# An encoder trunk on one core: the gated attention output turned by transposing DMAs instead of TensorE, and the joins of turned tiles queued behind weight casts

## The chip, the cores and the metric

The kernel runs on one core of one Trainium2 chip. The metric is the device time of one execution in microseconds. All times "at" some point are microseconds from the start of the profiled span. The engines are TensorE (PE, its weight loads PEld), VectorE (DVE), ScalarE (ACT), GpSimd (POOL) and SyncE (SP), which here only issues DMAs.

## The reference

256 tokens of width 1024 go through two layers. What matters here:

```python
u = rms_norm(h, g_mix_pre)
(gq, gk, gv, gg, ra_f, ra_b, aq, ak, av, gate_a, gate_b) = jnp.split(u @ w_in, offsets, axis=-1)
...
o_gla = rms_norm(o_f + o_b, g_gla_out).reshape(b, s, GLA_VAL).astype(h.dtype)
branch_a = (o_gla * jax.nn.silu(gg)) @ w_o_gla
...
branch_b = gqa_attention(q, k, v) @ w_o_attn
mixed = jax.nn.sigmoid(gate_a) * branch_a + jax.nn.sigmoid(gate_b) * branch_b
h = h + rms_norm(mixed @ w_out, g_mix_post)
```

Then follow a gated FFN of 2816 hidden units (`w_ffn_in`, silu, `w_ffn_out`), its norm and residual, and the layer's input embedding, `h += rms_norm(sigmoid(h @ w_ple_gate) * (p[i] @ w_ple_proj))`. Everything is 32-bit floating point.

## The kernel before, in words

**Tiles and precision.** The tokens are two halves (`hf` 0 and 1) of 128 partitions. A matmul takes its activations turned, 128 features on the partitions by the tokens, as the stationary operand; the weights stream as the moving operand, 512 columns at a time. To keep 32-bit accuracy each operand is split (`split`, L132 to 134) into a high part, a cast on ACT, and a low part, a subtraction on DVE; a product is three matmuls (high x high, high x low, low x high), so that one 512-column result of four 128-feature steps is a group of 12 matmuls. `Split` holds a turned activation: its high and low tiles, and `makers`, the tasks that still have to make parts of it.

**Weights.** `Stream` (L248 on) brings the weights in units of 1 MB: a DMA on SP's queue into `raw` (two buffers; some units of the gates and the FFN go into `lent` or `big` tiles), then two casts into `wh` on ACT and two subtractions into `wl` on DVE (`fill`, `made`, four buffers each). Gate B and pairs of FFN blocks are computed with seven products in place of eight (`seven`, L713; the sums of weights stand on L326 to L332).

**Order of the work.** The program is traced in one order, and a scheduler places each engine's instructions by it, by priorities (`tc.high_priority`) and by `tc.issue_after`, which puts an instruction behind a named one on the same engine. A `Task` (its code is a generator) is work for later: it yields a number of ticks, and a `tick` comes after every six matmuls or so of the main stream, 1.36 us. What it makes is demanded at the latest by `need`, where a matmul uses it.

**Turning by TensorE.** `transpose_in` (L445) turns 128 x 128 blocks by TensorE (L449) into a PSUM tile `aux`, and splits it from there (L134). The gated output of branch A is made in `out_gate` (L1451): `sg`, the sigmoid of `gg`, times `gg` and `on`, one 128 x 1024 tile for each half. `turn_in` (L557) makes a task that turns it after `W["g"]` = 6 ticks, into `gT`, which the first merge unit (`w_o_gla`) multiplies. Four tiles of four transposes per layer, `aux_0gg` and `aux_1gg`.

**Turning by DMA.** The FFN's hidden activations `hid` are turned by a DMA (`turned` L1573, `turn_out` L455, `take_in` L472), which handles only 16-bit elements: ACT copies a 32-bit tile into two planes of its upper and lower halves (L468), SP issues one `dma_start_transpose` (L469, 128 x 8 x 128 elements), and after `WAIT_TURNED` = 9 ticks ACT joins the turned planes into 32-bit values (L476), which are then split. Planes and turned planes lie in halves of a fresh `mid` tile. Block pairs make one such tile for each half (k = 4, 12, 16); the last pair (k = 16) is turned by TensorE. Single blocks (k = 0, 8, 10, 20) have both halves in one tile or, for the first, one tile for each half.

## Time and profile before

| | |
|---|---|
| median of three runs | 908.5 us (908.41 to 908.8) |
| the profiled execution's own time | 909.68 us |
| its span | 907.9 us |
| granted clock of TensorE | 0.999 |

The span is the stretch from the first to the last recorded instruction; the profiled execution took 1.8 us more than its span and 1.2 us more than the median. A row of the timeline gives the start, the time until the end of the last of its instructions, the engine, the line, the operation, the tiles (without their numbers) and the count; in square brackets stands how long the engine was idle before it, and what ended the wait. Matmuls overlap in the pipeline, so their cost is read from the distance of starts.

### The profile page before, as it was taken

Reading aid. Unit: us, or ns where it says so; the run is one execution under the profiler, and the core shown is the slowest. Engines: PE = TensorE matmul, PEld = TensorE weight load, DVE = VectorE, ACT = ScalarE, POOL = GpSimd, SP = SyncE. Lnnn points to the kernel's source line nnn. Section 1 sums busy time; section 2 is a strip of 40 time slices with the busy share of each in tenths; the row PEclk is TensorE's granted clock in tenths of the full one; section 3 lists DMA queues with packets and bytes.
Section 4 is the critical chain, followed back from the end, with each engine's and each line's share of the span. In section 5 each row is a group of like instructions: output and inputs, shape, how many; then the busy total and the mean of one; then the engine's idle time right before and its main releaser. Section 6 shows DMA issues by size and latency. Waiting matters only on the chain.

```text
span 907.9 us, 12157 instructions
## 1 busy us (share of the span) xinstructions
PE 898.8 (99%) x4479; PEld 762.2 (84%) x4479; DVE 790.2 (87%) x1021; ACT 620.5 (68%) x1011; POOL 105.9 (12%) x157
## 2 busy tenths in 40 slices
PE   9999999999999999999999999999999999999997
PEld 8898888888888887887898888888888888888886
DVE  7999989987668999998779899799876799999984
ACT  7688677564467787756676687675644796958563
POOL 3700221300100000000254001110000000000001
PEclk9999999999999999999999999999999999999999
DMA  8663445657397594956576424455573966858461
GB/s 283 219 189 136 140 140 191 216 187 249 115 288 204 173 301 146 317 170 233 180 279 204 168 93 140 139 186 185 186 241 100 309 180 206 254 210 264 150 231 47
DMA packets 108519, 178.16 MB, mean 196 GB/s; under 512 B 22494, under 2 KB 46566, under 8 KB 107948
## 3 DMA queue, kind: packets, MB, share of 16 engines
q1 hardware_dynamic: 108300, 177.25, 59.9%
q8 instruction: 35, 0.57, 0.3%
q14 instruction: 24, 0.20, 0.1%
q10 hardware_dynamic: 160, 0.14, 0.0%
HBM read 169.50 MB, written 3.15 MB: 190 GB/s over the span
## 4 chain that ended last, share of the span: by engine, by line
PE 78%; DVE 11%; DMA 4%; issue 4%; ACT 2%; POOL 0%; SPq 0%; POOLq 0%; ACTq 0%; DVEq 0%
PE acc_1ffnin L122 12%; PE acc_0gate L122 7%; PE acc_1gate L122 7%; PE acc_1ffnin L106 7%; DVE wl_0ffnin L134 6%; PE acc_1rq L122 3%; PE acc_0gqk L106 2%; PE acc_1gqk L106 2%; PE acc_1wout L122 2%; PE acc_0ple L122 2%; PE acc_1v L122 2%; PE acc_0gg L122 2%; PE acc_1gg L122 2%; PE acc_0v L122 2%; PE acc_0merge L122 2%
## 5 line engine op out<-in xcount | busy, mean ns | idle before, releaser
L134 ACT CAST wh_0ffnin<-raw_0ffnin 128x1024 fp32r<-128x1024 f32 x38 | 38.1, 1048 | 19.8 <-DMA raw_0ffnin<-in_w_ffn_out_dram 10.2
L134 ACT CAST wh_1ffnin<-raw_1ffnin 128x1024 fp32r<-128x1024 f32 x38 | 38.3, 1048 | 17.4 <-DMA raw_1ffnin<-in_w_ffn_out_dram 5.0
L134 DVE TENSOR_TENSOR wl_0ffnin<-raw_0ffnin,wh_0ffnin 128x1024 fp32r<-128x1024 f32 x38 | 44.6, 1219 | 5.8 <-ACT wh_0ffnin L134 5.8
L134 DVE TENSOR_TENSOR wl_1ffnin<-raw_1ffnin,wh_1ffnin 128x1024 fp32r<-128x1024 f32 x38 | 44.8, 1219 | 5.0 <-ACT wh_1ffnin L134 4.9
L106 PE MATMUL acc_0ffnin<-wh_0ffnin,big_0ffnin 128*128 128x512 f32 x176 | 45.4, 392 | 0.0
L106 PE MATMUL acc_1ffnin<-wh_1ffnin,big_1ffnin 128*128 128x512 f32 x176 | 45.1, 390 | 0.0
L122 PE MATMUL acc_0ffnin<-wh_0ffnin,big_0wout 128*128 128x512 f32 x168 | 41.8, 390 | 0.0
L122 PE MATMUL acc_1ffnin<-wh_1ffnin,big_1wout 128*128 128x512 f32 x168 | 41.5, 389 | 0.0
L106 PEld LDWEIGHTS acc_0ffnin<-wh_0ffnin,big_0ffnin 128*128 128x128 f32 x176 | 32.8, 188 | 7.5 <-DVE big_0ffnin L134 0.5
L106 PEld LDWEIGHTS acc_1ffnin<-wh_1ffnin,big_1ffnin 128*128 128x128 f32 x176 | 33.0, 188 | 6.9
L122 PEld LDWEIGHTS acc_0ffnin<-wh_0ffnin,big_0wout 128*128 128x128 f32 x168 | 31.4, 188 | 7.1 <-ACT wh_0ffnin L134 0.4
L122 PEld LDWEIGHTS acc_1ffnin<-wh_1ffnin,big_1wout 128*128 128x128 f32 x168 | 31.5, 188 | 6.5
L134 DVE TENSOR_TENSOR wl_1ffnin<-lent_1ffnin,wh_1ffnin 128x1024 fp32r<-128x1024 f32 x30 | 35.7, 1217 | 0.6 <-ACT wh_1ffnin L134 0.6
L134 DVE TENSOR_TENSOR wl_0ffnin<-lent_0ffnin,wh_0ffnin 128x1024 fp32r<-128x1024 f32 x30 | 35.6, 1216 | 0.1
L134 ACT CAST wh_1ffnin<-lent_1ffnin 128x1024 fp32r<-128x1024 f32 x30 | 30.7, 1051 | 5.4 <-PE acc_1ffnin L106 3.9
L134 ACT CAST wh_0ffnin<-lent_0ffnin 128x1024 fp32r<-128x1024 f32 x30 | 30.4, 1053 | 3.6 <-DVE lent_0ffnin L332 3.4
L134 ACT CAST wh_0gate<-raw_0gate 128x1024 fp32r<-128x1024 f32 x20 | 19.9, 1049 | 14.4 <-DMA raw_0gate<-in_w_o_attn_dram 6.1
L134 ACT CAST wh_1gate<-raw_1gate 128x1024 fp32r<-128x1024 f32 x20 | 19.9, 1048 | 13.9 <-PE acc_1gate L122 5.9
L134 DVE TENSOR_TENSOR wl_0gate<-raw_0gate,wh_0gate 128x1024 fp32r<-128x1024 f32 x20 | 24.2, 1257 | 5.2 <-ACT wh_0gate L134 5.1
L134 DVE TENSOR_TENSOR wl_1gate<-raw_1gate,wh_1gate 128x1024 fp32r<-128x1024 f32 x20 | 23.5, 1221 | 5.1 <-ACT wh_1gate L134 5.1
L106 PE MATMUL acc_0ffnin<-wl_0ffnin,big_0ffnin 128*128 128x512 f32 x88 | 24.6, 394 | 0.6 <-DVE wl_0ffnin L134 0.6
L106 PE MATMUL acc_1ffnin<-wl_1ffnin,big_1ffnin 128*128 128x512 f32 x88 | 24.0, 391 | 0.0
(730 smaller groups left out, 2731.7 us busy)
## 6 DMA issues: line engine op xcount, KB each, us to landing
raw_0ffnin<-in_w_ffn_out_dram SPq DMA_DIRECT2D x11, 1024.0 KB, 5.9
raw_1ffnin<-in_w_ffn_out_dram SPq DMA_DIRECT2D x11, 1024.0 KB, 5.5
lent_0ffnin<-in_w_ffn_in_dram SPq DMA_DIRECT2D x6, 1024.0 KB
lent_1ffnin<-in_w_ffn_in_dram SPq DMA_DIRECT2D x6, 1024.0 KB, 7.5
raw_0v<-in_w_in_dram SPq DMA_DIRECT2D x4, 1024.0 KB, 5.8
raw_0gate<-in_w_o_gla_dram SPq DMA_DIRECT2D x4, 1024.0 KB, 6.8
raw_0gate<-in_w_o_attn_dram SPq DMA_DIRECT2D x4, 1024.0 KB, 5.2
raw_0wout<-in_w_ffn_in_dram SPq DMA_DIRECT2D x8, 512.0 KB, 4.6
```

Of the source, the lines that this page charges most:

```text
L106: return nc.tensor.matmul(o, lhsT, rhs, start=start, stop=stop)
L122: nc.tensor.matmul(o, x, y, start=start and n == 0, stop=stop and n == len(seq) - 1, **kw)
L134: return nc.scalar.copy(hi, src), nc.vector.tensor_tensor(out=lo, in0=src, in1=hi.bitcast(F32), op=ALU.subtract)
```

## The change

It has three parts.

1. **The gated output is turned by DMAs.** `out_gate` calls `turn_out` for both 512-column halves of `sg`: the planes are written over `gg`, which is no longer needed, and the transposing DMA writes back over `sg`. A task for each half then waits 9 (half 0) or 11 (half 1) ticks (`WAIT_GATED`) and joins and splits, with one tick between its two parts. Per layer, 16 PE transposes go; four plane copies, four transposing DMAs and four joins come.
2. **Joins and transfers are queued.** `Stream` notes its last weight cast on ACT, its last subtraction on DVE and its last load on SP into an ordinary slot; `turn` puts joins and their splits behind the first two, and transposing DMAs behind the third. In the FFN the waits of k = 4 become 14 and 18 ticks, that of k = 20 becomes 22, the others stay at 9.
3. **In place.** In the FFN, too, the DMA writes back over its source tile, and the planes share `mid` tiles by halves.

The diff, cut to its core:

```diff
 WAIT_SPREAD = 12
-W = dict(r=5, z=6, s0=4, s=3, s1=9, o0=1, o=1, k=4, q=3, a0=1, a1=4, a2=4, a3=1, g=6)
+W = dict(r=5, z=6, s0=4, s=3, s1=9, o0=1, o=1, k=4, q=3, a0=1, a1=4, a2=4, a3=1)
+WAIT_GATED = 9, 11
 STEPS_FIRST = "00 10 01 11 02 12 03 13".split()
...
 OUT = (0, 1, 2, 3, 4, 5, 10, 6, 7, 8, 9)
-WAIT_TURNED, WAIT_LAST = 9, (3, 4)
+WAIT_TURNED, WAIT_LAST = {4: (14, 18), 20: 22}, (3, 4)
 GATES = "uuu1u2m34m5m67m"
...
             self.loads, self.jobs, self.lend, self.last = [], [], False, {}
+            self.queue = {}
             pairs = {}
...
                     if self.open:
-                        nc.sync.dma_start(dst, src)
+                        load = nc.sync.dma_start(dst, src)
+                        if not x.own:
+                            self.queue["SP"] = load
                     else:
...
             for piece in self.put(x):
-                split(*piece)
+                self.queue["ACT"], self.queue["DVE"] = split(*piece)
         def step(self, n, x, y, z, q):
...
                 for piece in pieces or ():
-                    self.last[n] = split(*piece)
+                    self.last[n] = self.queue["ACT"], self.queue["DVE"] = split(*piece)
                 if pieces:
                     self.load()
+
+        def turn(self, *engines):
+            stack = ExitStack()
+            for e in engines:
+                if e in self.queue:
+                    stack.enter_context(tc.issue_after(self.queue[e].ins))
+            return stack
         def behind(self, n, which):
...
             nc.scalar.copy(plain, ps[:, : n * P])
-    def turn_out(src, k, hf):
+    def turn_out(src, parts, mixed=False):
         with tc.high_priority(AHEAD):
-            both, turned = halves(mid())
-            turned = turned.bitcast(U16)
-            parts = both.bitcast(U16).rearrange("p (s c) -> p s c", s=2)
-            words = src.bitcast(U16)
-            if hf is None:
+            planes, words = (t.bitcast(U16) for t in (parts, src))
+            if mixed:
                 nc.scalar.copy(
-                    parts.rearrange("p s (k h f) -> p s k h f", k=2, f=P),
+                    planes.rearrange("p (s k h f) -> p s k h f", s=2, k=2, f=P),
                     words.rearrange("p (h k f s) -> p s k h f", h=2, f=P, s=2),
                 )
             else:
-                nc.scalar.copy(parts, words.rearrange("p (c s) -> p s c", s=2))
-            nc.sync.dma_start_transpose(out=turned.rearrange("p (x t) -> p x t", t=P), in_=parts.rearrange("p s c -> p (s c)"))
-        return both, turned
-
-    def take_in(sp, both, turned, k, hf):
-
-        n, tn = (2, T) if hf is None else (4, P)
-        hi, lo = sp.at(k, n, (hf or 0) * P, tn)
-        nc.scalar.copy(
-            both.bitcast(U16).rearrange("p (k t s) -> p k t s", s=2, t=tn),
-            turned.rearrange("p (s k t) -> p k t s", s=2, t=tn),
-        )
-        split(hi, lo, both.rearrange("p (k t) -> p k t", t=tn))
+                nc.scalar.copy(planes.rearrange("p (s c) -> p s c", s=2), words.rearrange("p (c s) -> p s c", s=2))
+        with ws.turn("SP"):
+            nc.sync.dma_start_transpose(out=words.rearrange("p (x t) -> p x t", t=P), in_=planes)
+
+    def take_in(hi, lo, src, parts):
+
+        tn = hi.shape[-1]
+        with ws.turn("ACT", "DVE"):
+            nc.scalar.copy(
+                parts.bitcast(U16).rearrange("p (k t s) -> p k t s", s=2, t=tn),
+                src.bitcast(U16).rearrange("p (s k t) -> p k t s", s=2, t=tn),
+            )
+            split(hi, lo, parts.rearrange("p (k t) -> p k t", t=tn))
     last_pow = [None]
...
                     vmul(t, t, on[:, hf, s])
-                turn_in(gT, sg, hf, W["g"])
+                xs = [(t, gg[:, hf, j * 512 : (j + 1) * 512]) for j, t in enumerate(halves(sg))]
+                for x in xs:
+                    turn_out(*x)
+
+                def turn(hf=hf, xs=xs):
+                    for j, x in enumerate(xs):
+                        yield WAIT_GATED[hf] if j == 0 else 1
+                        take_in(*gT.at(4 * j, 4, hf * P, P), *x)
+
+                gT.makers[hf].append(Task(turn(), part[0]))
         ogate = Task(out_gate(), f"{l}gg")
...
         part[0] = f"{l}ffnin"
-        hid = Split()
+        hid, spare = Split(), []
         us = [[ws.take() for _ in range(2)] for _ in range(2)]
...
                 else:
-                    x = turn_out(src, k, hf)
-                    yield WAIT_TURNED
-                    take_in(hid, *x, k, hf)
+                    if not spare:
+                        spare.extend(halves(mid()))
+                    parts = spare.pop()
+                    turn_out(src, parts, hf is None)
+                    wait = WAIT_TURNED.get(k, 9)
+                    yield wait if isinstance(wait, int) else wait[hf]
+                    take_in(*(hid.at(k, 2, 0, T) if hf is None else hid.at(k, 4, hf * P, P)), src, parts)
             t = Task(turn(), part[0], k // 4)
```

What it moves, engine by engine; a name ends in two numbers of which the first is the tile's. In the gate stage of layer 0, PE had the following. `acc_0gate` is gate A's sum, `wh_0gg` and `wl_0gg` the parts of its weights:

```order
L122 MATMUL acc_0gate_248_1599<-wh_0gg_231_1464,big_start_46_303 128x512 x8
L122 MATMUL acc_0gate_248_1599<-wl_0gg_232_1465,big_start_46_303 128x512 x4
L449 MATMUL aux_0gg_267_1714<-ident_87,mid_0gg_254_1636 128x128 x4
L449 MATMUL aux_0gg_269_1722<-ident_87,mid_0gg_254_1636 128x128 x4
L449 MATMUL aux_0gg_271_1730<-ident_87,mid_0gg_255_1642 128x128 x4
L449 MATMUL aux_0gg_272_1737<-ident_87,mid_0gg_255_1642 128x128 x4
L122 MATMUL acc_0gate_277_1755<-wh_0gg_245_1590,big_start_22_149 128x512 x8
L122 MATMUL acc_0gate_277_1755<-wl_0gg_246_1591,big_start_22_149 128x512 x4
```

and now has:

```order
L123 MATMUL acc_0gate_248_1599<-wh_0gg_231_1464,big_start_46_303 128x512 x8
L123 MATMUL acc_0gate_248_1599<-wl_0gg_232_1465,big_start_46_303 128x512 x4
L123 MATMUL acc_0gate_271_1733<-wh_0gg_245_1590,big_start_22_149 128x512 x8
L123 MATMUL acc_0gate_271_1733<-wl_0gg_246_1591,big_start_22_149 128x512 x4
L123 MATMUL acc_0gate_272_1734<-wh_0gg_245_1590,big_start_22_149 128x512 x8
L123 MATMUL acc_0gate_272_1734<-wl_0gg_246_1591,big_start_22_149 128x512 x4
```

The four rows of transposes are gone, and gate A's matmuls move up; the same holds for layer 1. ACT had at that place (264 the first unit of gate B's seven products, 274 and 279 the following gate units, 285 the first merge unit of `w_o_gla`; `big_0gg` from `aux_0gg` are the splits of the gated output):

```order
L134 COPY wh_0gate_264_1680<-lent_0gate_259_1670 128x1024 x2
L134 COPY wh_0gate_274_1747<-raw_0gate_262_1676 128x1024 x2
L134 COPY big_0gg_268_1719<-aux_0gg_267_1714 128x4x128
L134 COPY big_0gg_270_1727<-aux_0gg_269_1722 128x4x128
L134 COPY big_0gg_268_1719<-aux_0gg_271_1730 128x4x128
L134 COPY big_0gg_270_1727<-aux_0gg_272_1737 128x4x128
L1475 ACTIVATE big_0gate_273_1744<-acc_0gate_247_1598,rs_start_9_120 128x512
L1475 ACTIVATE big_0gate_273_1744<-acc_0gate_248_1599,rs_start_10_121 128x512
L134 COPY wh_0gate_279_1781<-big_0gate_260_1672 128x1024 x2
L134 COPY wh_0gate_285_1805<-raw_0gate_263_1678 128x1024
L740 COPY mid_0gate_281_1788<-acc_0gate_283_1790 128x512
L134 COPY wh_0gate_285_1805<-raw_0gate_263_1678 128x1024
```

and now has these (L476 copies into planes, L484 joins; 264, 268 and 275 are the gate units, 281 the first merge unit):

```order
L476 COPY big_0gg_201_1276<-mid_0gg_254_1636 128x1024 x2
L135 COPY wh_0gate_264_1688<-lent_0gate_259_1678 128x1024
L476 COPY big_0gg_201_1276<-mid_0gg_255_1646 128x1024 x2
L135 COPY wh_0gate_264_1688<-lent_0gate_259_1678 128x1024
L1492 ACTIVATE big_0gate_267_1722<-acc_0gate_247_1598,rs_start_9_120 128x512
L1492 ACTIVATE big_0gate_267_1722<-acc_0gate_248_1599,rs_start_10_121 128x512
L135 COPY wh_0gate_268_1725<-raw_0gate_262_1684 128x1024 x2
L484 COPY big_0gg_201_1276<-mid_0gg_254_1636 128x1024 x2
L135 COPY big_0gg_273_1753<-big_0gg_201_1276 128x4x128
L135 COPY big_0gg_274_1763<-big_0gg_201_1276 128x4x128
L135 COPY wh_0gate_275_1767<-big_0gate_260_1680 128x1024 x2
L484 COPY big_0gg_201_1276<-mid_0gg_255_1646 128x1024 x2
L135 COPY big_0gg_273_1753<-big_0gg_201_1276 128x4x128
L135 COPY big_0gg_274_1763<-big_0gg_201_1276 128x4x128
L748 COPY mid_0gate_277_1774<-acc_0gate_279_1776 128x512
L135 COPY wh_0gate_281_1797<-raw_0gate_263_1686 128x1024 x2
```

The planes are copied around unit 264, half 0 is joined after unit 268, half 1 after 275, and the first merge unit's casts come behind all of them. On SP the four transposing DMAs stand behind the load of `lent_0gate` (261) and ahead of that of the first merge unit; on DVE the four low parts of the gated output move from ahead of a sum of weights (L326) to behind the low parts of units 268 and 275.

In the embedding gate of layer 0 PE had the following; `acc_0ple` numbered 3964 and 3965 are the sums of half 0, 4065 of half 1:

```order
L122 MATMUL acc_0ple_623_3965<-wh_0ffnout_602_3928,big_0ffnout_598_3899 128x512
L1022 MATMUL aux_1emb_624_3984<-ident_87,mid_0ffnout_610_3950 128x128 x4
L449 MATMUL aux_0ffnout_625_4003<-ident_87,h_76 128x128 x4
L449 MATMUL aux_0ffnout_626_4010<-ident_87,h_76 128x128 x4
L122 MATMUL acc_0ple_623_3965<-wh_0ffnout_602_3928,big_0ffnout_598_3899 128x512 x7
L122 MATMUL acc_0ple_623_3965<-wl_0ffnout_603_3929,big_0ffnout_598_3899 128x512 x4
L122 MATMUL acc_0ple_636_4065<-wh_0ffnin_579_3776,big_0ffnout_596_3891 128x512
L122 MATMUL acc_0ple_636_4065<-wl_0ffnin_580_3777,big_0ffnout_596_3891 128x512
```

and now (3952 and 3953 half 0, 4053 half 1):

```order
L123 MATMUL acc_0ple_614_3952<-wh_0ffnout_591_3896,big_0ffnout_590_3887 128x512 x4
L123 MATMUL acc_0ple_628_4053<-wh_0ffnin_571_3764,big_0ffnout_588_3879 128x512
L123 MATMUL acc_0ple_628_4053<-wl_0ffnin_572_3765,big_0ffnout_588_3879 128x512
L123 MATMUL acc_0ple_615_3953<-wh_0ffnout_594_3916,big_0ffnout_590_3887 128x512 x4
L123 MATMUL acc_0ple_628_4053<-wh_0ffnin_571_3764,big_0ffnout_588_3879 128x512
L123 MATMUL acc_0ple_628_4053<-wl_0ffnin_572_3765,big_0ffnout_588_3879 128x512
L123 MATMUL acc_0ple_628_4053<-wh_0ffnin_571_3764,big_0ffnout_588_3879 128x512
L123 MATMUL acc_0ple_628_4053<-wl_0ffnin_572_3765,big_0ffnout_588_3879 128x512
L123 MATMUL acc_0ple_628_4053<-wh_0ffnin_571_3764,big_0ffnout_588_3879 128x512
L123 MATMUL acc_0ple_628_4053<-wl_0ffnin_572_3765,big_0ffnout_588_3879 128x512
L123 MATMUL acc_0ple_628_4053<-wh_0ffnin_571_3764,big_0ffnout_588_3879 128x512 x2
L123 MATMUL acc_0ple_615_3953<-wh_0ffnout_594_3916,big_0ffnout_590_3887 128x512 x4
```

Matmuls of half 1 stand ahead of the last ones of half 0. In the FFN's output steps matmuls of both halves mix in other places, the joins stand behind casts, and the transposing DMAs a load or two later; the numbers of instructions there are the same.

## The prediction

> **What bounds the kernel now.** I read the engine shares and the granted clock first, then what TensorE waited for, because a removed matmul is worth its time only if nothing else would fill the hole.
>
> ```profile
> span 907.9 us, 12157 instructions
> ...
> PE 898.8 (99%) x4479; PEld 762.2 (84%) x4479; DVE 790.2 (87%) x1021; ACT 620.5 (68%) x1011; POOL 105.9 (12%) x157
> ...
> PEclk9999999999999999999999999999999999999999
> ```
>
> TensorE (PE) is busy 99% of the span, at the full granted clock in every slice. The list of its waits, in us in total, times and longest, has four entries:
>
> ```profile
> PE warm L106 <- POOL seed L143: 1.0, 1, 1.0
> PE acc_0ffnin L106 <- DVE wl_0ffnin L134: 0.6, 2, 0.3
> PE acc_0ffnin L122 <- DVE wl_0ffnin L134: 0.2, 1, 0.2
> PE aux_0ffnout L449 <- DVE h L611: 0.2, 1, 0.2
> ```
>
> So TensorE bounds every stage, and it hardly waits: 0.8 us in the FFN is all that better spaced casts could give back. Work taken from TensorE shortens the span by its length, as long as what feeds the next matmuls comes sooner too. The feeders are ScalarE (ACT) and VectorE (DVE), which make each weight's high and low part, and SyncE's queue (SP), which loads them.
>
> **What is removed.** Per layer, 16 PE transposes of the gated output. The weight-load side shows their slot, and what an ordinary group of 12 matmuls takes (two starts of "x8" rows):
>
> ```profile
> 146.56 0.87 PEld L122 LDWEIGHTS acc_0gate<-wl_0gg,big_start 128*128 128x128 f32 x4
> 147.47 1.90 PEld L449 LDWEIGHTS aux_0gg<-ident,mid_0gg 128*128 128x128 f32 x16
> ...
> 162.85 1.77 PEld L122 LDWEIGHTS acc_0gate<-wh_0gate,mid_0gate 128*128 128x128 f32 x8
> 164.66 0.87 PEld L122 LDWEIGHTS acc_0gate<-wl_0gate,mid_0gate 128*128 128x128 f32 x4
> 165.57 1.77 PEld L122 LDWEIGHTS acc_0gate<-wh_0gate,big_0gg 128*128 128x128 f32 x8
> ```
> ```profile
> 146.78 1.07 PE L122 MATMUL acc_0gate<-wl_0gg,big_start 128*128 128x512 f32 x4
> 147.70 1.91 PE L449 MATMUL aux_0gg<-ident,mid_0gg 128*128 128x128 f32 x16
> ...
> 151.28 1.07 PE L122 MATMUL acc_0gate<-wl_0gg,big_start 128*128 128x512 f32 x4
> ```
>
> A group of 12 takes 165.57 − 162.85 = 2.72 us. The two "wl" rows around the transposes stand 151.28 − 146.78 = 4.50 us apart, where one group alone would make it 2.72. So the 16 transposes cost 1.78 us. The stage of the second layer has the same 16 with the same row:
>
> ```profile
> L449 PE MATMUL aux_0gg<-ident,mid_0gg x16: 271/272/273, 147.7 to 149.3; 128*128 128x128 f32 x16
> L449 PE MATMUL aux_1gg<-ident,mid_1gg x16: 271/272/273, 603.5 to 605.2; 128*128 128x128 f32 x16
> ```
>
> Two layers: **−3.56 us**. One transpose has a duration of 272 ns, but they are pipelined, and the slot counts. The Trainium skill (TensorE: Matmul & The Clock Gate, Part 4: PE-mode transpose) gives about 275 ns for a transpose within a kernel; the 272 ns agree, but 32 of them one after another would be 8.8 us, an estimate from that page that the slot of 1.78 us per 16 contradicts.
>
> **What is added: ScalarE.** Each layer gets four copies into 16-bit planes and four joins; the eight splits stay. The nearest rows are the FFN's, same shape:
>
> ```profile
> L476 ACT COPY mid_0ffnin<-mid_0ffnin 128x1024 uint16<-128x1024 uint16 x9 | 10.5, 1177 | 12.0 <-DMA mid_0ffnin<-mid_0ffnin 12.0
> ...
> L468 ACT COPY mid_0ffnin<-t_0ffnin 128x1024 uint16<-128x1024 uint16 x6 | 6.3, 1044 | 0.8 <-DVE t_0ffnin L127 0.8
> ```
>
> That is 4 × 1.044 + 4 × 1.177 = 8.9 us per layer, in the stretch where ScalarE was doing this:
>
> ```profile
> 143.46 2.00 ACT L134 CAST wh_0gate<-lent_0gate 128x1024 fp32r<-128x1024 f32 x2 [0.55 <-DMA lent_0gate<-in_w_in_dram]
> 146.98 2.00 ACT L134 CAST wh_0gate<-raw_0gate 128x1024 fp32r<-128x1024 f32 x2 [1.51 <-PE acc_0gate L122]
> 148.89 2.04 ACT L134 CAST big_0gg<-aux_0gg 128x512 fp32r<-128x512 f32 x4
> 150.80 1.29 ACT L1475 ACTIVATE big_0gate<-acc_0gate,rs_start 128x512 f32<-128x512 f32 x2
> 154.20 2.01 ACT L134 CAST wh_0gate<-big_0gate 128x1024 fp32r<-128x1024 f32 x2 [2.11 <-PE acc_0gate L122]
> 156.92 1.06 ACT L134 CAST wh_0gate<-raw_0gate 128x1024 fp32r<-128x1024 f32 x1 [0.71 <-PE acc_0gate L122]
> 157.88 0.58 ACT L740 COPY mid_0gate<-acc_0gate 128x512 f32<-128x512 f32 x1
> 158.36 1.06 ACT L134 CAST wh_0gate<-raw_0gate 128x1024 fp32r<-128x1024 f32 x1
> ```
>
> The cast at 156.92 is the first merge unit, which meets the gated output in the matmuls of 165.57. It stood some 7 us ahead of need; in the new order it stands behind all eight copies. I replayed the new ACT order. The outputs of half 0 are done in DVE's row of 143.70, so ACT starts at about 144.45:
>
> ```profile
> 143.70 1.28 DVE L127 TENSOR_TENSOR mid_0gg<-mid_0gg,big_0gla 128x512 f32<-128x512 f32 x2
> ...
> 146.11 1.28 DVE L127 TENSOR_TENSOR mid_0gg<-mid_0gg,big_0gla 128x512 f32<-128x512 f32 x2
> ```
>
> Back to back, an instruction counts by its pitch: 0.95 for a cast (two from 146.98 to 148.89), 0.48 for a split or small copy, 0.6 for a sigmoid, and some 0.1 under their duration for copies (0.94) and joins (1.08). Plane copies of half 0 to 146.3; first half of the cast 264 to 147.3; plane copies of half 1 (ready 147.4) to 149.2; other half of 264 to 150.1; two sigmoids to 151.3; 268 to 153.2; joins and splits of half 0 to 156.3; 275 to 158.2; those of half 1 to 161.3; a small copy to 161.8; the halves of 281 to 162.75 and 163.7. TensorE, 1.78 us sooner, wants the first at 163.8 and the second about 0.45 us later: it fits, by 0.5 to 1 us. At full durations instead of pitches the halves end at 165.0 and 166.0, 1.2 and 1.8 us late: the whole saving. So the stall is 0 to 1.8 us per layer; I take 0.3, near the pitches, since such runs of instructions do stand at their pitch in the rows above. After that unit ACT catches up in the 2.7 us per group against some 2 us of casts.
>
> **VectorE** has the same splits, moved behind the weights' subtractions and a sum of two weights:
>
> ```profile
> 156.59 2.35 DVE L134 TENSOR_TENSOR wl_0gate<-raw_0gate,wh_0gate 128x1024 fp32r<-128x1024 f32 x2
> ...
> 161.13 2.28 DVE L329 TENSOR_TENSOR lent_0gate<-lent_0gate,big_0gate 128x2048 f32<-128x2048 f32 x1
> ```
>
> Replayed alike, each behind its cast, the low part of 281 ends at 164.7 and 165.8 against needs of 165.6 (1.8 us into the group) and 166.0: within the 0.3.
>
> **SP.** Four transposing DMAs per layer now stand ahead of the load of that first merge unit, which SP issued at 142.01:
>
> ```profile
> 142.01 0.37 SPq L297 DMA_DIRECT2D raw_0gate<-in_w_o_gla_dram  x1
> ```
> ```profile
> L469 SPq DMA_TRANSPOSE mid_0ffnin<-mid_0ffnin x9: 1237/1250/1922, 268.3 to 377.1; - x9
> ...
> DMA to landing us min/median/max: 3.3/3.6/4.3
> ```
> ```profile
> raw_0gate<-in_w_o_gla_dram SPq DMA_DIRECT2D x4, 1024.0 KB, 6.8
> ```
>
> SP takes 1.25 us to issue each; the last waits for the plane copies that end at 149.2, so the load goes out at about 150.5, 8.5 us later, and lands at 157.3. ACT reads it at 161.8: 4.5 us to spare. Half 0's planes land at about 151.5 (join at 153.2), half 1's at 154 (join at 158.2). Cost nothing, hidden by the eight ticks' work; without the cover each us late is a us of stall.
>
> **FFN.** The same copies, joins and transposes in other places: joins queue behind the casts, transposes behind loads. ACT's wait at the head of its queue for landing planes (12.0 us, row above) shrinks, and so may the 0.8 us of TensorE's waits; but a join that is pushed too late stalls an output step. The joins with the longest waits, of k=4 half 1, come 2 ticks (2.7 us) ahead of use. I bound it by −0.8 and +0.8 and take −0.3.
>
> **The embedding gate of layer 0.** The scheduler also puts 11 of half 1's matmuls among half 0's last 12: half 0's gate ends 11/12 × 2.72 = 2.5 us later. Behind it stands the next layer's norm and transposes:
>
> ```profile
> 448.89 1.28 DVE L127 TENSOR_TENSOR mid_0ple<-h,mid_0ple 128x512 f32<-128x512 f32 x2
> ```
> ```profile
> 453.67 1.04 PE L449 MATMUL aux_0ple<-ident,mid_0ple 128*128 128x128 f32 x8
> ```
>
> The data was ready at 450.2, 3.5 us ahead; 2.5 of that go, and up to half of a 1.2 us subtraction comes between. 0 to 1 us; I take 0.2.
>
> **Sum.** The profiled run took 909.68 us, 1.8 over its span and 1.2 over the median of 908.5. 909.68 − 3.56 + 2 × 0.3 − 0.3 + 0.2 = 906.6; against the median, **905.4**.
>
> **Rivals.**
> (a) *ScalarE is the new bound* at the first merge unit: the full durations hold, 1.8 us per layer, and the saving is gone: 908.5. Against it stand the pitches; for it, the margin of half a microsecond and the semaphore of each dependent step. Half of it gives 907.
> (b) *Slower: the transposes land one after another.* Four stand in a row, where the FFN has at most two. If each takes its 3.6 us behind the one before, from 145.5 on, the last lands at 159.9, and the load that is queued behind lands 6.8 later, at 166.7, with its cast 1.9 us more: 168.6 and a join late before that, against 164.2. That is 4.4 us per layer: 908.5 − 3.6 + 8.8 = 913.7. It decides from a landing of the load after 162.3 + 1.8 = 164 on. Against it: SP can issue every 1.25 us, and landing took 4.3 at most. The Trainium skill (VectorE: DVE Perf Modes, The three transpose paths and Rules for kernel authors) says to use TensorE for a 128x128 transpose where PSUM will do as destination, the crossbar's DMA otherwise, with 390 against 1309 ns. By it one of these DMAs, eight such tiles, would be an estimated 10.5 us, and this change much slower; the 3.3 to 4.3 us per DMA here disagree, so its size stays out and only its sign is in (b).
> (c) *The FFN's waits go as well*, and no stall comes: 908.5 − 3.56 − 0.8 = 904.1.
> (d) *Nothing happens*, because the transposes lay in time that TensorE had to spare. The 99% and the waits exclude it: under 0.02, within "same".
>
> **Chances.** Forecast (903.9 to 906.7) 0.57; (c) and beyond 0.12; (a) 0.17, of which 0.05 are still faster by over 0.2%; (b) and like it, with a late join in the FFN, 0.14. 0.2%, or 1.8 us, is about what a measurement of this kernel can tell from no change. Faster 0.74, same 0.12, slower 0.14. The range goes from 903.3, a little under (c), to 909.5, past (a), and leaves out most of (b) and the tail of (c).
>
> **What would show it.** Right: no aux_0gg or aux_1gg rows, the group rows of 2.72 us follow each other through 147 to 149, no new entry in TensorE's waits, ACT's casts of the merge unit just ahead of their matmuls. Wrong by (a): a wait of acc_0gate for wh_0gate or wl_0gate of 1 to 2 us per layer, with ACT busy without a gap before it. Wrong by (b): ACT idle for a DMA ahead of the gated output's joins or of that cast. An FFN or embedding-gate wait of over 1 us would make those two terms wrong.

## The result, and the profile after

| | before | after |
|---|---|---|
| median, runs on the same chip | 909.11 us (907.96 to 911.03, 22 runs) | 910.42 us (908.84 to 912.03, 22 runs) |
| ratio | | 1.0016, 95% interval 1.0009 to 1.0022 |
| profiled execution and its span | 909.68, 907.9 us | 911.55, 909.5 us |

The prediction of 905.4 us (903.3 to 909.5, "faster" at 0.74) was wrong, in its range and in its sign: the change costs 0.1 to 0.2%. The head of the page of after, to be held against the two rows of before: 32 instructions fewer on TensorE, 2.1 us less of busy time, and a longer span.

```profile
span 909.5 us, 12114 instructions
...
PE 896.7 (99%) x4447; PEld 757.6 (83%) x4447; DVE 791.2 (87%) x1021; ACT 633.4 (70%) x1027; POOL 104.6 (12%) x157
```

**The stage of the change did what was forecast.** After's weight loads at layer 0's gates (start, time, engine):

```profile
158.33 1.77 PEld L123 LDWEIGHTS acc_0gate<-wh_0gate,big_start 128*128 128x128 f32 x8
...
161.05 1.77 PEld L123 LDWEIGHTS acc_0gate<-wh_0gate,mid_0gate 128*128 128x128 f32 x8
...
163.77 1.77 PEld L123 LDWEIGHTS acc_0gate<-wh_0gate,big_0gg 128*128 128x128 f32 x8
```

Groups follow each other at 2.72 us, no bracket (no idle time) stands behind a row, and the first group of the merge unit starts at 163.77; the forecast had 163.8, before had 165.57. ScalarE's replay held to a few tenths as well:

```profile
153.13 2.24 ACT L484 COPY big_0gg<-mid_0gg 128x1024 uint16<-128x1024 uint16 x2
...
158.21 2.25 ACT L484 COPY big_0gg<-mid_0gg 128x1024 uint16<-128x1024 uint16 x2
...
161.88 2.01 ACT L135 CAST wh_0gate<-raw_0gate 128x1024 fp32r<-128x1024 f32 x2
```
```profile
145.46 6.18 SPq L478 DMA_TRANSPOSE mid_0gg<-big_0gg  x4
151.69 0.58 SPq L299 DMA_DIRECT2D raw_0gate<-in_w_o_gla_dram  x1
```

Joins at 153.1 and 158.2, the cast at 161.9 (forecast 153.2, 158.2, 161.8), the load at 151.7 (forecast 150.5), and nothing waits for a transfer.

**The loss lies elsewhere.** The rows of weight loads of the two runs, matched one by one without the transposes that went, give the difference of their starts. TensorE is level up to 139 us, 1.8 us ahead at 160 and 176, 0.6 at 248, 2.0 at 327, 1.1 at 406 and 1.2 at 458; then it is 0.7 behind at 466, 1.0 ahead again behind layer 1's gates (634), 0.9 behind at 727 and 1.7 behind at the last match (900). TensorE's list of waits, four rows before, now has nine:

```profile
PE acc_1rq L123 <- DVE wl_0ple L135: 1.4, 2, 0.8
...
PE aux_1wout L460 <- DVE mid_1wout L552: 1.0, 1, 1.0
PE acc_0ffnin L107 <- DVE wl_0ffnin L135: 1.0, 1, 1.0
...
PE acc_1ffnin L107 <- DVE wl_1ffnin L135: 0.4, 1, 0.4
PE acc_0ple L123 <- DVE wl_0ffnout L135: 0.3, 1, 0.3
```

The largest loss, 1.9 us from 458 to 466 us, stands behind layer 0's embedding gate. In the weight loads and VectorE's rows of after:

```profile
464.39 0.19 PEld L123 LDWEIGHTS acc_1rq<-wl_0ple,big_0ple 128*128 128x128 f32 x1 [0.85 <-DVE wl_0ple L135]
465.56 0.19 PEld L123 LDWEIGHTS acc_1rq<-wl_0ple,big_0ple 128*128 128x128 f32 x1 [0.99 <-DVE wl_0ple L135]
```
```profile
460.55 1.41 DVE L619 SCALAR_TENSOR_TENSOR h<-mid_0ple,rstd_0ple,h 128x512 f32<-128x512 f32 x2 [1.33 <-POOL rstd_0ple L548]
461.88 1.29 DVE L128 TENSOR_TENSOR mid_0ple<-h,mid_0ple 128x512 f32<-128x512 f32 x2
463.09 2.42 DVE L135 TENSOR_TENSOR wl_0ple<-raw_0ple,wh_0ple 128x1056 fp32r<-128x1056 f32 x2
```

And VectorE's rows of before:

```profile
459.41 1.26 DVE L134 TENSOR_TENSOR wl_0ple<-raw_0ple,wh_0ple 128x1056 fp32r<-128x1056 f32 x1 [1.22 <-ACT wh_0ple L134]
...
460.92 1.25 DVE L134 TENSOR_TENSOR wl_0ple<-raw_0ple,wh_0ple 128x1056 fp32r<-128x1056 f32 x1
462.95 1.42 DVE L611 SCALAR_TENSOR_TENSOR h<-mid_0ple,rstd_0ple,h 128x512 f32<-128x512 f32 x2 [0.78 <-POOL rstd_0ple L540]
```

Here `h` is the residual behind half 1's norm. In before two low parts of the next layer's first weights stand ahead of it on VectorE; in after they stand behind it, although ScalarE began their casts at 458.62. VectorE waits 1.33 us for the norm (`rstd`), and TensorE 0.85 and 0.99 us for the two low parts. Of all the traces only after's and e2's (below) have both of them behind the residual, and only these two have the wait.

Some 30 us earlier SyncE's queue of after has another order of loads:

```profile
426.32 0.39 SPq L1022 DMA_DIRECT2D mid_0ffnout<-in_p_dram  x1
431.48 0.37 SPq L299 DMA_DIRECT2D raw_0ffnout<-in_w_ple_gate_dram  x1
...
437.23 0.37 SPq L299 DMA_DIRECT2D raw_0ffnout<-in_w_ple_proj_dram  x1
```

In before the same loads went out earlier and the input embedding behind them:

```profile
429.31 0.37 SPq L297 DMA_DIRECT2D raw_0ffnout<-in_w_ple_gate_dram  x1
433.31 0.37 SPq L297 DMA_DIRECT2D raw_0ffnout<-in_w_ple_proj_dram  x1
433.73 0.46 SPq L1014 DMA_DIRECT2D mid_0ffnout<-in_p_dram  x1
```

The weights of the embedding's gate and projection go out 2.2 and 3.9 us later. They are not what acc_1rq waits for: those weights went out at 453.17 us against 452.47. The other trace of the change is in the transposing DMAs themselves (nanoseconds at SyncE, min/median/max; then us from issue to landing):

```profile
L478 SPq DMA_TRANSPOSE t_0ffnin<-mid_0ffnin x9: 1231/1463/4229, 267.2 to 376.8; - x9
L478 SPq DMA_TRANSPOSE t_1ffnin<-mid_1ffnin x9: 1232/1239/4262, 721.3 to 827.2; - x9
...
DMA to landing us min/median/max: 3.0/5.0/8.4
```

Before, the issue took 1.9 us at most and the landing 3.3/3.6/4.3. Now a transposing DMA holds the queue for up to 4.26 us, and its data lands up to 8.4 us after the issue.

Two rows of before that I had not read. First, the weight loads of layer 0's FFN, with their idle time:

```profile
294.43 0.77 PEld L122 LDWEIGHTS acc_0ffnin<-wh_0ffnin,big_0wout 128*128 128x128 f32 x4 [0.45 <-ACT wh_0ffnin L134]
...
296.33 0.30 PEld L122 LDWEIGHTS acc_0ffnin<-wl_0ffnin,big_0wout 128*128 128x128 f32 x2 [0.67 <-DVE wl_0ffnin L134]
...
342.36 0.30 PEld L106 LDWEIGHTS acc_0ffnin<-wl_0ffnin,big_0ffnin 128*128 128x128 f32 x2 [0.78 <-DVE wl_0ffnin L134]
```

All such brackets of before between 255 and 428 us add up to 5.05 us, where the list of matmul waits, whose ends are modelled, has 1.0 in all. In layer 1's FFN (705 to 882 us) they are only 0.34 us. Second, the busy time by stretches (length, then PE, PEld, DVE, ACT):

```profile
255.00:428.00 173.00, 171.81 (x760) 139.41 (x759) 156.04 (x154) 125.98 (x156) 2.43 (x5) 1.00 0.71 222
284.00:300.00 16.00, 15.74 (x68) 12.26 (x67) 16.00 (x16) 12.62 (x17) 0.00 (x0) 1.00 0.50 101
330.00:348.00 18.00, 17.65 (x78) 14.24 (x78) 18.00 (x17) 17.35 (x23) 0.00 (x0) 1.00 0.78 236
378.00:406.00 28.00, 28.00 (x126) 23.17 (x125) 27.94 (x24) 20.18 (x24) 0.00 (x0) 1.00 0.56 172
```

VectorE, 87% over the whole span and 90% over layer 0's FFN (156.04 of 173 us), has no gap in the three shorter stretches: 16.00 of 16, 18.00 of 18, 27.94 of 28 us. There two engines are full at once, and VectorE has no time to make up for a late cast; e13 below follows one such delay on to TensorE.

### The profile page after: what moved, and what is told of

It is laid out like the page before. It is cut to its first block, busy times and chain, and to the rows that moved or that the text cites. A ratio compares the mean times of both kernels' runs of the same rounds, so it can differ in the third digit from the quotient of the medians.

```text
span 909.5 us, 12114 instructions
## 1 busy us (share of the span) xinstructions
PE 896.7 (99%) x4447; PEld 757.6 (83%) x4447; DVE 791.2 (87%) x1021; ACT 633.4 (70%) x1027; POOL 104.6 (12%) x157
## 4 chain that ended last, share of the span: by engine, by line
PE 70%; DVE 13%; DMA 5%; ACT 5%; issue 4%; POOL 2%; SPq 0%; POOLq 0%; ACTq 0%; DVEq 0%
PE acc_1ffnin L123 9%; PE acc_1gate L123 7%; PE acc_0ffnin L123 6%; PE acc_1ffnin L107 6%; DVE wl_0ffnin L135 5%; PE acc_0gqk L107 2%; PE acc_1gqk L107 2%; PE acc_1v L123 2%; PE acc_1gg L123 2%; PE acc_0v L123 2%; PE acc_1merge L123 2%; PE acc_0merge L123 2%; PE acc_1rq L123 2%; PE acc_1ple L123 2%; PE acc_0wout L123 2%
```

## The experiments

All ratios are to the kernel before on the same chip, with 95% intervals. Executions of one kernel differ by 1 to 7 us, and some profiled runs (e5 and e8 by 2.2 and 2.7 us, e9, e11, e12 and e14 by 0.9 to 1.0) start late, in the first 20 us, so traces are compared by stage and times by ratio.

### Which half: e1 and e2

e1: the FFN's tasks call the old functions again, with their wait of 9.

```diff
-                    turn_out(src, parts, hf is None)
-                    wait = WAIT_TURNED.get(k, 9)
-                    yield wait if isinstance(wait, int) else wait[hf]
-                    take_in(...)
+                    x = turn_out_old(src, k, hf)
+                    yield 9
+                    take_in_old(hid, *x, k, hf)
```

> Only the gated output is turned by DMAs, with its joins and transfers queued as in the change; the FFN's turns are as before (own mid tiles, nine ticks, joins not queued). PE's order is that of before without the 32 transposes. Theory A (the loss comes from the FFN's half of the change, by way of the scheduler's new order in layer 0's embedding gate): the 3.56 us show, ratio to before about 0.996, some 905.5 us where before has 909.1, and acc_1rq does not wait for wl_0ple. Theory B (a head start of TensorE is eaten again at the next place where a weight load or a norm is late, whatever the order): ratio 0.999 to 1.001, with new waits behind the gate stage. Theory C (the gated output itself costs: copies and joins delay casts): ratio 1.000 or over, with waits of acc_0gate or acc_1gate.

Measured: 907.49 us (906.25 to 910.69, 11 runs), ratio 0.9982 (0.9972 to 0.9992).

e2: the gated output is turned by TensorE again, the FFN half stays.

```diff
-                xs = [(t, gg[:, hf, j * 512 : (j + 1) * 512]) for j, t in enumerate(halves(sg))]
...
-                gT.makers[hf].append(Task(turn(), part[0]))
+                turn_in(gT, sg, hf, 6)
```

> Only the FFN's half of the change: in-place planes, waits of 14, 18 and 22 ticks, joins behind casts and transfers behind loads; the gated output is turned by TensorE as before. Theory A: slower than before by about what the change lost, some 5 us (ratio 1.004 to 1.006), with the 1 to 2 us wait of acc_1rq for wl_0ple. Theory B: ratio 0.999 to 1.002, since there is no head start to eat and no TensorE work is added. Theory C: ratio 0.999 to 1.000.

Measured: 913.89 us (911.83 to 915.98, 6 runs), ratio 1.0049 (1.0035 to 1.0064), and the wait of acc_1rq of 1.4 us is there too, with VectorE's order of after; 1.9 us of e2's loss arise there, from 458 to 466 us. The gate half is a gain, the FFN half a loss of some 4.5 us.

### First guesses at the FFN half: e3 to e6

e3 takes the queueing out of `turn` (`if False:`), for the gated output too; the transposes still have no raised priority. e4 sets all waits to 9 (`WAIT_TURNED = {}`).

> The whole change, but joins and transposing DMAs are not put behind weight casts, subtractions and loads; ticks and in-place planes stay. PE's order is again that of before without the 32 transposes, so layer 0's embedding gate has its old order. Theory A: close to e1, ratio 0.995 to 0.998. Theory B: ratio 0.999 to 1.001. Theory C: ratio 1.000 or over, since the copies and joins of the gated output are all there, and joins at the head of ACT's queue may wait for landing planes.

> The whole change with nine ticks for every FFN join instead of 14, 18 and 22; the queueing stays. PE's order differs from before in the FFN's output steps, and in the embedding gate of layer 0 by a few rows only, not by the 11 matmuls. Theory A: the loss there is mostly gone, ratio 0.996 to 0.999, unless the earlier joins stall FFN casts. Theory B: ratio about 1.000 to 1.002, as the change. Theory C: as the change, 1.001 to 1.002.

Measured: e3 911.44 us (907.65 to 914.52, 9 runs), 1.0023 (1.0008 to 1.0038); e4 910.88 us (909.18 to 914.41, 12 runs), 1.0023 (1.0013 to 1.0034). Neither gives the gain back, so neither guess was the cause by itself. Looking back, e3 doesn't undo the transfers' place, as e13 below shows.

e5 and e6 (the change, and e2) forbid TensorE's interleaving in layer 0's embedding gate, with a constraint behind half 0's last matmul:

```diff
+            if hf == 1 and apart:
+                after_mm[0] = last_mm[0]
...
-        by_half(hT, after_gate, l + 1 == DEPTH)
+        by_half(hT, after_gate, l + 1 == DEPTH, l == 0)
```

> The whole change and one constraint: in layer 0's embedding gate no matmul of half 1 is issued ahead of half 0's last. From the next layer's first projection on, all engines then have the order of before. Theory A (that order costs the change some 2 us at acc_1rq, and up to 1 us ahead of it): ratio to before 0.998 to 1.000, the change itself standing at 1.0016, and no wait of acc_1rq for wl_0ple. Theory B (whatever TensorE wins is eaten later): ratio 1.001 to 1.002, with the 2 us turning up as a wait in layer 1's FFN.

> The FFN's half of the change alone, as in e2, with the same constraint in the embedding gate; the gated output by TensorE. Theory A: about 2 to 2.5 us less than e2's 1.0049, so 1.002 to 1.003: what is left is the FFN's own cost. If the order were harmless: 1.004 to 1.006, as e2.

Measured: e5 912.45 us (910.18 to 916.61, 10 runs), 1.0030 (1.0017 to 1.0044); e6 915.63 us (914.97 to 917.23, 6 runs), 1.0065 (1.0053 to 1.0078). Not better: e5 stands 0.14% above the change and e6 0.16% above e2, each within what the intervals allow, and in their traces the wait of acc_1rq is gone but another has come. The weight loads of e5 (e6 has the same wait, 2.08 us):

```profile
444.73 0.76 PEld L126 LDWEIGHTS acc_0ple<-wh_0ffnout,big_0ffnout 128*128 128x128 f32 x4 [2.09 <-ACT wh_0ffnout L138]
```

The scheduler's 11 matmuls filled a wait for a late weight; without them TensorE stands still. Forbidding the interleaving gains nothing, so by itself it is not what costs the time.

### What the gate half is worth: e7 and e8

e7 is the kernel before without the transposes of the gated output and with nothing in their place: it splits `sg` unturned, so that the turning is left out. e8 makes each of the 32 transposes twice. The edits, e7's first:

```diff
-                turn_in(gT, sg, hf, W["g"])
+                def turn(hf=hf, sg=sg):
+                    yield W["g"]
+                    for j, y in enumerate(halves(sg)):
+                        with tc.high_priority(AHEAD):
+                            gT.put(y, 4 * j, 4, hf * P, P)
+                gT.makers[hf].append(Task(turn(), part[0]))
```
```diff
-                turn_in(gT, sg, hf, W["g"])
+                turn_in(gT, sg, hf, W["g"], times=2)
...
-        for i in range(n):
+        for i in list(range(n)) * times:
```

> Before, without the 32 transposes of the gated output and with nothing in their place: the splits read the output unturned, so the turning is left out. It has none of the added copies, joins and DMAs. If each us off TensorE's path is a us off the end: ratio 0.9960 (3.56 us). Theory B: less, 0.997 to 0.999, close to e1's 0.9982, with weight loads waiting in the FFN for casts that do not come sooner. Theory C (the copies and joins are what cost e1 the rest): 0.9960, clearly under e1.

> Before, with each of the 32 transposes of the gated output done twice, so 3.56 us more on TensorE and nothing else. If TensorE bounds every stage: ratio 1.0039. Theory B: less, 1.002 to 1.003, since the delay takes the place of waits for casts in the FFN that before has.

Measured: e7 908.95 us (907.07 to 912.61, 12 runs), 0.9988 (0.9975 to 1.0001); e8 913.93 us (913.66 to 914.52, 5 runs), 1.0045 (1.0033 to 1.0057). By the ratios, adding 3.56 us costs about 4.1, and taking 3.56 us away without anything in its place gives 1.1. The first doesn't show that all of it lasts to the end. e8's trace is 2.7 us late by 20 us, before the doubled transposes. They cost 1.74 us at layer 0's gates and 1.73 at layer 1's, but from 248 to 430 us 3.1 us come back, where before's weight loads stood idle (in the FFN 5.05 us in before, 0.95 in e8); at the end it is 4.2 us late, 1.5 more than at 20 us. In e7 VectorE's splits come at once and stand ahead of the subtractions that TensorE now wants sooner:

```profile
158.21 0.30 PEld L122 LDWEIGHTS acc_0gate<-wl_0gate,big_start 128*128 128x128 f32 x2 [0.49 <-DVE wl_0gate L134]
159.35 0.30 PEld L122 LDWEIGHTS acc_0gate<-wl_0gate,big_start 128*128 128x128 f32 x2 [0.84 <-DVE wl_0gate L134]
```

So only 0.8 of the 1.78 us are gained there; layer 1's gates have the same two waits. Then follow 1.77 us for the load of the input embedding at 439 us. What TensorE gains is kept only where the feeders come sooner too. e1, which has the copies and joins, is no slower than e7; since e7 pays for its own order of splits, this doesn't show that they cost nothing.

### Three parts of the FFN half, one by one: e9 to e14

Each has e1's gate half. e9 adds part 3 of the FFN half, in place; the order of every engine is e1's. e10 adds the queueing only, into fresh tiles. e11 is e1 with the input embedding's load raised in priority, and has nothing of the FFN half. The edits in that order (e9 calls both functions from the FFN with `queue=False`, and e9 and e10 wait 9 ticks):

```diff
-        with ws.turn("SP"):
+        with ws.turn("SP") if queue else tc.high_priority(AHEAD):
-        with ws.turn("ACT", "DVE"):
+        with ws.turn("ACT", "DVE") if queue else ExitStack():
```
```diff
-                    parts = spare.pop()
-                    turn_out(src, parts, hf is None)
+                    parts, dst = halves(mid())
+                    turn_out(src, parts, hf is None, dst)
```
```diff
-        nc.sync.dma_start(pin, a["p"][l, 0].rearrange("(s p) c -> p s c", p=P))
+        with tc.high_priority(AHEAD):
+            nc.sync.dma_start(pin, a["p"][l, 0].rearrange("(s p) c -> p s c", p=P))
```

> The gated output by DMA as in e1, and of the FFN half of the change only part 3: the DMA writes back over its source tile and the planes share tiles. No queueing in the FFN, all waits 9 ticks, transposes with the priority of before. The order of every engine is that of e1; only tiles differ. Theory P (writing in place holds the source tiles longer and costs the FFN half its time): ratio 1.001 to 1.003 to the kernel before, like e3 and e4, with new idle time of weight loads in the FFN. Theory Q (the queueing of joins and transfers, and the longer waits, cost it): e1's ratio of 0.998 (0.997 to 0.999), and e1's waits.

> The gated output by DMA as in e1, and of the FFN half only the queueing: joins behind the last weight cast, transposes behind the last load, all waits 9 ticks, the DMA into a fresh tile. Theory Q: like e4, which differs by writing in place alone: ratio 1.001 to 1.003, with joins at later places of ScalarE's order and new idle time of weight loads for wl_0ffnin or wh_0ffnin. Theory P: e1's 0.998.

> e1 with one edit more: the load of the input embedding p has high priority, so that it goes out one load earlier on SyncE's queue; in e1 and e7 TensorE's weight loads stood still for it, 1.45 and 1.77 us at 437 to 439 us. Theory B (whatever TensorE gains is eaten where casts or loads come just in time): that wait goes, and 0.3 to 1.4 us of it stay: 906.1 to 907.2 on e1's chip, ratio 0.9965 to 0.998. If later stages eat it all: e1's 0.9982. If the earlier load delays the weights behind it (as in the changed kernel, where it goes out at 426 us): 0.999 or more, with a wait for wh_0ffnout or wl_0ple instead.

Measured: e9 906.85 us (905.45 to 911.57, 12 runs), 0.9964 (0.9950 to 0.9978); e10 912.03 us (910.28 to 915.35, 12 runs), 1.0017 (1.0004 to 1.0031); e11 907.67 us (906.03 to 909.76, 12 runs), 0.9968 (0.9956 to 0.9981). Writing in place costs nothing, the queueing costs all of it. e11 is not told apart from e9.

e12 queues only the joins, e13 only the transfers, e14 only lengthens the waits; each is e9 with that one edit, here in that order.

```diff
-                    take_in(*(...), src, parts, False)
+                    take_in(*(...), src, parts)
```
```diff
-                    turn_out(src, parts, hf is None, False)
+                    turn_out(src, parts, hf is None)
```
```diff
-WAIT_TURNED, WAIT_LAST = {}, (3, 4)
+WAIT_TURNED, WAIT_LAST = {4: (14, 18), 20: 22}, (3, 4)
```

> e9 and one part of the queueing: joins and their splits in the FFN stand behind the last weight cast on ScalarE and the last subtraction on VectorE; transfers are not queued, waits are 9. Theory Qj (a join that stands behind casts delays what comes behind it, the casts of the next units included): the cost of e10, ratio 1.001 to 1.003. Theory Qt (the transfers behind loads are it): e9's 0.9964 (0.995 to 0.998).

> e9 and the other part of the queueing: the FFN's transposing transfers stand behind the last load on SyncE's queue and have no raised priority; joins as before. TensorE's order is that of e9. Theory Qt (the transfer goes out some us later, behind a load that waits for its slot, and the join that waits for it at the head of ScalarE's queue holds up the casts): ratio 1.000 to 1.003, and ScalarE's idle time for landing planes grows over e9's. Theory Qj: e9's 0.9964.

> e9 and the waits of the change alone, 14 and 18 ticks for the joins of k=4 and 22 for that of k=20, nothing queued in the FFN. The orders of TensorE and SyncE are those of e9, and three joins stand later on ScalarE. If later joins cost nothing by themselves: 0.9964 (0.995 to 0.998). If the joins come too late for their output steps: 1.000 or more, with waits for the hidden activations or for the weights behind the joins.

Measured: e12 908.63 us (907.16 to 911.02, 12 runs), 0.9984 (0.9974 to 0.9994); e13 912.52 us (910.51 to 917.35, 12 runs), 1.0029 (1.0014 to 1.0044); e14 907.53 us (905.43 to 908.17, 6 runs), 0.9962 (0.9948 to 0.9976). One at a time, the transfers' place behind loads is the large cost, some 0.65% or 5.9 us against e9; the joins behind casts are a smaller one, 0.2%, at the edge of the intervals; the waits cost nothing alone. e13 also takes the transfers' raised priority away. e3, in which nothing is queued and only that priority is gone, has the same orders on TensorE and SyncE and 1.0023, so the lost priority alone moves the transfers behind the loads.

e9 and e13 have the same order on TensorE, so the chain can be followed. SyncE's order where the second block of a pair is turned, in e9 and then in e13:

```
106 L478 DMA_TRANSPOSE t_0ffnin_3434<-mid_0ffnin_3155 128x8x128
107 L478 DMA_TRANSPOSE t_0ffnin_3460<-mid_0ffnin_3463 128x8x128
108 L299 DMA raw_0ffnin_3445<-in_w_ffn_in_dram 128x4x512

105 L478 DMA_TRANSPOSE t_0ffnin_3434<-mid_0ffnin_3155 128x8x128
106 L299 DMA raw_0ffnin_3445<-in_w_ffn_in_dram 128x4x512
107 L478 DMA_TRANSPOSE t_0ffnin_3460<-mid_0ffnin_3463 128x8x128
```

The same place in time: SyncE, ScalarE and the landings of all transposes in e9:

```profile
373.11 5.23 SPq L478 DMA_TRANSPOSE t_0ffnin<-mid_0ffnin  x2
378.39 0.58 SPq L299 DMA_DIRECT2D raw_0ffnin<-in_w_ffn_in_dram  x1
```
```profile
379.64 2.24 ACT L484 COPY mid_0ffnin<-t_0ffnin 128x1024 uint16<-128x1024 uint16 x2 [1.19 <-DMA t_0ffnin<-mid_0ffnin]
...
382.83 2.00 ACT L135 CAST wh_0ffnin<-raw_0ffnin 128x1024 fp32r<-128x1024 f32 x2
```
```profile
DMA to landing us min/median/max: 3.1/3.1/3.4
```

And in e13, with VectorE and the weight loads as well:

```profile
375.11 0.51 SPq L299 DMA_DIRECT2D raw_0ffnin<-in_w_ffn_in_dram  x1
377.15 2.36 SPq L478 DMA_TRANSPOSE t_0ffnin<-mid_0ffnin  x1
```
```profile
384.17 1.17 ACT L484 COPY mid_0ffnin<-t_0ffnin 128x1024 uint16<-128x1024 uint16 x1 [2.06 <-DMA t_0ffnin<-mid_0ffnin]
385.25 1.99 ACT L135 CAST wh_0ffnin<-raw_0ffnin 128x1024 fp32r<-128x1024 f32 x2
```
```profile
386.32 2.36 DVE L135 TENSOR_TENSOR wl_0ffnin<-raw_0ffnin,wh_0ffnin 128x1024 fp32r<-128x1024 f32 x2 [1.74 <-ACT wh_0ffnin L135]
```
```profile
402.44 0.30 PEld L107 LDWEIGHTS acc_0ffnin<-wl_0ffnin,big_0ffnin 128*128 128x128 f32 x2 [0.67 <-DVE wl_0ffnin L135]
403.58 0.30 PEld L107 LDWEIGHTS acc_0ffnin<-wl_0ffnin,big_0ffnin 128*128 128x128 f32 x2 [0.84 <-DVE wl_0ffnin L135]
```
```profile
DMA to landing us min/median/max: 3.0/4.2/6.5
```

Read it as a chain. A 1 MB load of weights goes out 3.3 us sooner, ahead of a transposing DMA. The DMA takes 2.36 us to issue, and its planes are read at 384.2, 7.0 us after the issue began. The join waits 2.06 us at the head of ScalarE's queue, and the cast behind it starts 2.4 us later than in e9 (385.25 against 382.83; 0.6 of that e13 was late already at 374 us). VectorE, which has no gap in this stretch, waits 1.74 us for that cast and doesn't catch up; 16 us later TensorE waits for a low part, 0.67 and 0.84 us, where e9 has no wait. In layer 1 the same two waits come at 851 us; at 341 and 790 us, where e9 waits too, e13 waits 1.0 and 0.3 us longer. Idle weight loads outside the start add up to 13.3 us in e13 and 7.4 in e9, a difference as large as the measured one. ScalarE's waits for planes grow by 1.7 us in all (13.3 in e9, 15.0 in e13); it is their place that counts.

### Back in the whole change: e15, and the fastest mixture: e16

e15 is the change with the FFN's transposes ahead of the loads again, at their raised priority; e16 is e14 with e11's early load. The edit of e15 (the last argument is `queue`, as in e9):

```diff
-                    turn_out(src, parts, hf is None)
+                    turn_out(src, parts, hf is None, False)
```

> The whole change, with one part undone: the FFN's transposing transfers have their raised priority again and do not stand behind loads. If the transfers' place is what costs the change its gain: 0.997 to 0.9990 to the kernel before (e12 has 0.9984), no wait of acc_1rq for wl_0ple. If the joins behind casts and their longer waits cost as much in this mixture: 1.001 or more, as the changed kernel's 1.0016.

> e14 (gated output by DMA, in place, the longer waits, nothing queued in the FFN) with the early load of the input embedding of e11. Both alone were 0.9962 and 0.9968. If the wait for that load is worth something beside e14's order: 0.995 to 0.996. If what it saves is eaten further on, as between e9 and e11: 0.996 to 0.997.

Measured: e15 909.84 us (908.11 to 915.26, 12 runs), 0.9996 (0.9979 to 1.0013); e16 906.25 us (904.62 to 907.03, 6 runs), 0.9954 (0.9937 to 0.9970). Undoing the transfers' place alone gives back some 0.2%, or 1.8 us (1.0016 to 0.9996, with an interval that allows from nothing to 0.4%). VectorE's order and the wait of acc_1rq, worth 1.9 us, are gone from e15's trace.

That is less than e13's 0.65%, and the chain of e13 does not explain after: there the joins stand behind casts, and none of them waits for its planes. The transfers' place costs 0.65% where joins aren't queued (e13 against e9, waits for planes 15.0 us), 0.39% where they are (e4 against e12, waits 2.7 us) and 0.2% where they also wait longer (after against e15, no waits). The rest of the loss, 0.32% from e9 to e15, is the joins' queue together with the longer waits; which of their places costs it is not settled. e16 has the lowest ratio of all, though the intervals don't tell it from e9, e11 and e14: the gated output by DMA, the FFN in place with the longer waits, nothing of the FFN queued, the input embedding loaded one step earlier.

Where after's loss stands can be read against e9's trace, each counted from its own start: of 4.3 us between the two, 1.6 have arisen by 430 us, 2.0 arise in and behind layer 0's embedding gate up to 466 us, and 0.7 after it.

## Why the prediction was wrong, point by point

- **What bounds the kernel.** "TensorE bounds every stage, and it hardly waits" is the step that failed. It took a share of the whole span (VectorE 87%) for every stage, and the list of matmul waits (0.8 us in the FFN) for all of TensorE's waiting. In stretches of the FFN VectorE is as full as TensorE, and the weight loads of layer 0's FFN alone were idle for 5.05 us. So "0.8 us in the FFN is all that better spaced casts could give back" was too small by several us, and in the full stretches worse spaced casts had no room at all.
- **−3.56 us for the transposes** was right: the slot of 1.78 us per layer is gone in full at the gates in the traces of after and of e1, and doubling the work costs the same there (e8). That it reaches the end in full does not follow: e1 ends 1.6 us faster than before, e9 3.3, and e8's delay partly fills before's own waits.
- **ScalarE's stall of 0.3 us per layer**: there is none at the merge unit, so rival (a) did not happen. What follows is of another kind: 1.06 us at 183 to 186 us in layer 0 of after, for a cast ahead of which ScalarE stands idle 6.66 us for a load. All kernels with the gate half have it (1.0 to 1.1 us) but e1; layer 1 has none.
- **SP at the gates, rival (b)**: four transposes were issued in 6.18 us, nothing waited for them. Not (b).
- **The sum of the gate half**, −3.56 + 0.6 = −2.96 us, is a ratio of 0.9967; e1, e9, e11 and e14, which have it with nothing of the FFN queued, gave 0.9982, 0.9964, 0.9968 and 0.9962. Had the change been this half, the result would have lain in the stated range, with e1's gain just over half of the one forecast.
- **FFN −0.3 us (bounds −0.8 and +0.8) and embedding gate +0.2 (0 to 1)** are the terms that were mis-sized, in sign and size. e2 measures the half they stand for at +0.49%, or 4.5 us; after against e9 says 0.52%. I put down "transposes behind loads" as a gain, because ScalarE's wait of 12.0 us for landing planes would shrink. It did (0.0 in after), and it was worth nothing: e12 has none of it either and is no faster than e9, which waits 11.3 us there. One cost left out is the place of the transfers: their landing, 3.6 us before, became 5.0 with a maximum of 8.4. Where joins wait for it, this is the 0.65% of e13; in the change itself no join waits, and undoing the place gives 0.2%. The other 0.3% go with the joins' queue and the longer waits, and there the cause stays open.
- **The embedding gate itself.** I priced half 0's norm, which could come behind a subtraction, and that was right: from 430 to 458 us after loses 0.1 us. I did not ask what half 1's norm would hold up: the low parts stand behind its residual on VectorE, and TensorE waits 1.84 us for them. The term of 0.2 (0 to 1) left this wait out. The 11 matmuls that I took as the cost were the scheduler's answer to a late weight: e5 and e6 took them away and did not get faster.
- **(c)** had the waits of the FFN go as well. Some of before's did (at 294 to 296 us after gains 0.9), and others came. **(d)** is excluded by e1.
- The last line on what would show it wrong, "an FFN or embedding-gate wait of over 1 us", is what the trace of after shows: 1.42 us for wl_0ffnin at 341 us and 1.84 for wl_0ple by the weight loads (1.0 and 1.4 in the list of matmul waits).

## What to carry to other kernels

Ask by stretches, not over the span, which engine has no gap, and read TensorE's waits from its weight loads: a second engine that is full has no time to make up for a delay of what feeds it. When a change queues a small transfer behind a large one, price the landing of the small one again, and ask who stands behind it; in e13, where joins wait for it at the head of ScalarE's queue, this cost more than the 3.56 us of 32 transposes. When the scheduler changes an order, look at both sides of each pair that came close. And test a change by its parts: this one was a gain of 0.2 to 0.4% and a loss of 0.5% in one diff.

## What the runs showed of the hardware

- A transposing DMA of 128 x 8 x 128 16-bit elements in the FFN takes SyncE 1.24 us to issue when it stands ahead of loads (e9, medians 1.237 in both layers, at most 1.77) and up to 4.26 behind them (after). With the gates' own it lands 3.1 us after its issue in the one case (e9, maximum 3.4; up to 5.6 in e12 and e15) and after 5.0, at most 8.4, in the other (after).
- 16 more pipelined 128 x 128 transposes lengthen the slot by the same 1.8 us as the first 16; the weight-load row of e8 for layer 0:

```profile
150.19 3.65 PEld L449 LDWEIGHTS aux_0gg<-ident,mid_0gg 128*128 128x128 f32 x32
```

- Time that TensorE loses ahead of a wait can come back: of the 1.74 us that e8's doubled transposes cost at layer 0's gates and the 2.7 us that it started late, 3.1 us were gone again by 430 us.
- In some profiled runs TensorE gets through its first matmuls later, up to 2.7 us (e8) at 20 us from the start, before any edit of these kernels acts; two single profiles don't settle a difference smaller than that by their ends. What delays them is not known.
